# Rotated query tiles between the plain ones, the last attention-output tiles by token half, and the first gate and up products slice by slice

## The chip, the cores and the metric

The kernel runs on one core of a Trainium2 chip. The metric is the time of one execution on the device in microseconds (us). A core has five engines that run side by side, each through its own list of instructions in order: TensorE (PE, matmuls and the weight loads for them), VectorE (DVE), ScalarE (ACT), GpSimd (POOL) and SyncE (SP, which issues DMAs; ACT and POOL issue some too). They meet through semaphores. Matmuls write to PSUM, which has eight banks of 128x512 float32 here, and the other engines read them from there.

## The reference

One transformer block over 1024 tokens of width 1024, in float32: adaLN conditioning, one input projection, then two branches side by side (attention with a low-rank query and key/value, and a state-space scan), sigmoid gates, an output projection and a SwiGLU feed-forward network, each half closed by an RMS norm and a residual.

```python
q = (rms(q_lat) @ w_uq).reshape(s, 8, 64 + 32)
q_nope, q_rope = q[..., :64], rope(q[..., 64:])
kv = rms(kv_lat); k_nope = kv @ w_uk; v = kv @ w_uv
o = softmax(scale * (q_nope @ k_nope.T + q_rope @ k_rope.T)) @ v
branch_a = o @ w_attn_out
mixed = (gate_a * branch_a + gate_b * branch_b) @ w_mix_out
x = x + gt1 * rms(mixed)
h = rms(x) * (1 + sc2) + sh2
g, up = split(h @ w_ffn_in)
x = x + gt2 * rms((silu(g) * up) @ w_ffn_out)
```

## The kernel before

All activations lie transposed, features on the partitions and tokens along the row, and the 1024 tokens are worked on as two halves of 512. To keep float32 accuracy every operand is split in a high part (rounded to the matmul's float32 format) and a low part (the rest), and `mm3` (L197) issues three matmuls for one 128x128 weight block: high weight with high data, high weight with low data, low weight with high data. PE takes them in the order in which they are written.

Weights come through one stream, `WStream`. A list `wl` says in which order the matrices are used. SP loads them (`load`), ACT casts the high part and DVE subtracts for the low part (`split`, L183 and the next line), and `get(ahead=1, more=2)` hands out the next matrix, after it has put the split of the matrix behind it into ACT's and DVE's lists. So a matrix is split where the matrix before it is fetched, unless `get` is told to look further ahead. The order of all lists is written out by hand; nothing is reordered later.

**Query tiles.** The query projection has six 128-row tiles, in three pairs of one weight matrix each: four plain ones (`uq_nope(i, w)`) and two that hold the rotated part (`uq_rope`). A tile takes 18 matmuls (two halves of nine). Its halves stand in two PSUM banks, one of four named `mm` and one of four named `s`, taken in turn. A plain tile is evicted by `split_store`: ACT scales and rounds the high part (`sghi`), DVE makes the low part (`sglo`), and both go to DRAM; five pairs of these buffers are in turn. `uq_rope` evicts with twelve DVE products and sums against the tables `csb` and four `split_store`s. Around them stand three generators, moved on by `next`: `kv_norm` (applies the norm to the key/value rows, in two token halves), `krope` (the rotated key; its row `kr` comes by a DMA of POOL's) and `ych` (loads the state-space output in `ylo`, then takes gelu on ACT, a cast to `yhi` on ACT, and a subtraction on POOL, four times). Then key and value tiles alternate: `uk_half` in a bank `mm`, `uv_tiles` in a bank `s`, six matmuls each, sixteen of them. Before, the order is plain 0, 1, 2, 3, then rotated.

**Attention output.** For eight output tiles m and two token halves h, `ao_mm` accumulates twelve matmuls (for m < 4 nine of them ahead), and `ao_out` evicts: DVE multiplies with the gate `ga`, adds the other branch `mb`, ACT casts the high part into `mxt[h]`, POOL makes the low part. `ga` and `mb` of a tile (both halves) are loaded two tiles ahead by `gm_load` into two buffers. The mix projection follows: `mix_tile(0, 0)` reads all eight slices of `mxt[0]`.

**Feed-forward.** Hidden tiles come in pairs of matrices, gate `wg` and up `wu`. For a token half h, `ffn_in` runs `prod` over the eight slices k of `h2t[h]` for gate (24 matmuls), then for up (24), with `tick()` after every second slice (it moves on the work of a `chain` and issues waiting DMAs). The slices of `h2t[h]` are made one after another by `chain(h)`; `drain()` ends that chain just ahead of the first pair of each half, so its last slices are still being made on DVE and ACT while PE is at that pair:

```python
        drain()                     # the rest of chain(h): eight slices
...
        wg, wu = win.get(), win.get()
```

The first `get` here puts the split of `wu` behind the chain's last slice in ACT's and DVE's lists, the second that of the next pair's `wg`.

Of the kernel before, what the change touches and what calls it, by code (L numbers as in the profile page):

```python
# [17 lines left out]
P = 128  # L18
S = 1024
D = 1024  # L20
KD = D // P
HF = 512
# [35 lines left out]
class Ops:  # L58
# [6 lines left out]
    def tt(self, o, a, b, op):  # L65
        return self.eng.tensor_tensor(o, a, b, op=op)  # L66
# [24 lines left out]
def _body(tc, a, out):  # L91
# [53 lines left out]
    def flush(keep=0):  # L145
        while len(pending) > keep:
            A_.dma_start(*pending.pop(0))
# [49 lines left out]
    def mm3(ps, w, rhi, rlo, k, first, last):  # L197

        whi, wlo = w
        c = slice(k * P, (k + 1) * P)  # L200
        PE.matmul(ps, whi[:, c], rhi, start=first, stop=False)  # L201
        PE.matmul(ps, whi[:, c], rlo, start=False, stop=False)  # L202
        PE.matmul(ps, wlo[:, c], rhi, start=False, stop=last)  # L203
# [89 lines left out]
            units += [("in", p, hs) for p in range(starts[g], starts[g + 1])] + [("out", g, hs)]  # L293

    wl = [(a["win"][i], KD * P) for i in range(26)]
    wl += [(a["wuq"][i], 6 * P) for i in range(3)] + [(a["wuk"], 8 * P), (a["wuv"], 2 * HF)]
    wl += [(a["wglu"][m], 8 * P) for m in range(KD)]
    wl += [(a["wao"][m], KD * P) for m in range(4)]
    mix0 = len(wl)
# [7 lines left out]
    win = WStream(wp, wl, D, (2, 3))  # L307
# [558 lines left out]
    def lat_apply(raw, rc, gcol, hi, lo, al, mk_ps):  # L866

        dg = [al(h) for h in range(2)]
        for h in range(2):
            norm_diag(rc[:, 4 * h:4 * h + 4], dg[h])  # L870
        yield
        rs = [al(2), al(3)]
        for h in range(2):
            ps = mk_ps()
            PE.matmul(ps, ones, dg[h], start=True, stop=True)
            A_.copy(rs[h], ps)
        yield

        def low(h, k):
            tt(lo[k][:, halves[h]], raw[k][h], hi[k][:, halves[h]].bitcast(F32), ALU.subtract)  # L880

        prev = None
        for h, c in enumerate(halves):
            for k in range(len(raw)):
                r = raw[k][h]
                stt(r, r, gcol[:, k:k + 1], rs[h], ALU.mult, ALU.mult)
                A_.copy(hi[k][:, c], r)
                if prev:
                    low(*prev)
                prev = h, k  # L890
            if h == 0:
                yield
        low(*prev)

    def load_rows(i):
        t = nr_tile()
        SY.dma_start(t, pdram[i])
        return [t[:, c] for c in halves]
# [106 lines left out]
    def dense_tile(w, i, kk, hi_in, lo_in):  # L1005

        pss = []
        for h, c in enumerate(halves):
            ps = (ps_mm, ps_s5)[h]()
            for k in range(kk):  # L1010
                mm3(ps, w, hi_in[k][:, c], lo_in[k][:, c], i * kk + k, k == 0, k == kk - 1)
            pss.append(ps)
        return pss
# [13 lines left out]
    kv_norm = lat_apply([load_rows(3), load_rows(4)], kv_rc[0], g_kv, kvhi, kvlo, lambda i: kv_scr[i], ps_mm)  # L1027
# [38 lines left out]
    def uq_nope(i, w):  # L1066
        pss = dense_tile(w, i % 2, 3, qhi, qlo)
        for c, ps in zip(halves, pss):
            split_store(ps, SCALE, [qkd["qn"][e, i * P:(i + 1) * P, c] for e in range(2)])

    def uq_rope():

        w = win.get(2)
        pss = [dense_tile(w, i, 3, qhi, qlo) for i in range(2)]
        qr = [qkd["qr"][e].rearrange("(h a r) s -> a h r s", a=2, r=16) for e in range(2)]
        yield
        prev = []
        for h, c in enumerate(halves):
            for i, op in enumerate((ALU.subtract, ALU.add)):
                ti = rp.tile([P, HF], F32, name="qra", tag="qra", bufs=3)  # L1080
                u = rp.tile([P, HF], F32, name="qrb", tag="qrb")
                tt(ti, pss[i][h], csb[0][:, c], ALU.mult)
                tt(u, pss[1 - i][h], csb[1][:, c], ALU.mult)
                tt(ti, ti, u, op)
                prev.append((ti, SCALE, [qr[e][i][:, :, c] for e in range(2)]))
                if len(prev) > 1:
                    split_store(*prev.pop(0))
            yield
        for p in prev:
            split_store(*p)  # L1090
# [47 lines left out]

    ych, krope = y_chain(), k_rope()
    next(krope)  # L1140
    for i in range(4):
        if i % 2 == 0:
            w = win.get()
        uq_nope(i, w)
        next(kv_norm, None)
        if i == 2:
            next(krope)
        if i == 2:
            next(ych)
    uqr = uq_rope()  # L1150
    next(uqr)
    for _ in kv_norm:
        pass
    next(ych)
    for _ in uqr:
        next(ych)
    w = win.get()
    uv = uv_tiles(win.get())
    for m in range(4):
# [87 lines left out]
    def mx_ps():  # L1247
        return psat.tile([P, S], F32, name="mx", tag="mx")
# [74 lines left out]
    for i in range(len(steps) + LAG):  # L1323
        if 0 <= i < len(steps):
            h, kt = steps[i]
# [4 lines left out]
        if NJ <= j < len(steps):  # L1330
            mh_, mt = steps[j]
            ps = mx_ps()
# [39 lines left out]
    def ps_b():  # L1372
        return psb.tile([P, HF], F32, name="mm", tag="mm")
# [5 lines left out]
    with ExitStack() as m_es:  # L1379
        mp = pool("mp", bufs=2, stack=m_es)  # L1380
        gm = {}

        def gm_load(m):
            if m < KD:
                gm[m] = [mp.tile([P, S], F32, name=n, tag=n) for n in ("ga", "mb")]
                later(gm[m][0], gdram[KD + m])
                later(gm[m][1], mbd[m])

        def ao_mm(ps, w, m, h, ks):
            o = m % 2 * 4  # L1390
            for k in ks:
                c = slice((o + k) * P, (o + k + 1) * P)
                for wi, x in ((0, ohi), (0, olo), (1, ohi)):
                    PE.matmul(ps, w[wi][:, c], x[k][:, halves[h]], start=(k == 0 and x is ohi and wi == 0),
                              stop=(k == 3 and wi == 1))

        def ao_out(ps, m, h):
            c = halves[h]
            ga, mb = gm[m]
            t = mp.tile([P, HF], F32, name="t", tag="t", bufs=4)  # L1400
            tt(t, ps, ga[:, c], ALU.mult)
            ao_low()
            tt(t, t, mb[:, c], ALU.add)
            A_.copy(mxt[h][0][:, m, :], t)  # L1404
            mlast.append((t, m, h))

        def ao_low():

            if mlast:
                t, m, h = mlast.pop()  # L1410
                hi, lo = mxt[h]
                G.tensor_tensor(lo[:, m, :], t, hi[:, m, :].bitcast(F32), op=ALU.subtract)

        mlast = []

        gm_load(0)
        gm_load(1)
        flush()
        w = [win.get(), win.get()]
        pss = {}  # L1420
        for m in range(4):
            for h in range(2):
                pss[m, h] = ps_b()
                ao_mm(pss[m, h], w[m // 2], m, h, range(3))
        for m in range(KD):
            if m >= 4 and m % 2 == 0:
                w = [win.get()]
            if m in (2, 4):
                win.split()
            for h in range(2):  # L1430
                if m < 4:
                    ps = pss[m, h]
                    ao_mm(ps, w[m // 2], m, h, (3,))
                else:
                    ps = ps_b()
                    ao_mm(ps, w[0], m, h, range(4))
                ao_out(ps, m, h)
            gm_load(m + 2)
            flush()
        ao_low()  # L1440
    o_es.close()
    v_es.close()
# [20 lines left out]
    def tick():  # L1463
        flush(FK)
        while backlog:
            try:
                next(backlog[0])
                return
            except StopIteration:
                backlog.pop(0)  # L1470
# [6 lines left out]
    def prod(ps, w, hi, lo, n, off=0):  # L1477
        for k in range(n):
            mm3(ps, w, hi(k), lo(k), off + k, k == 0, k == n - 1)
            if k % 2:  # L1480
                tick()

    def half_tile(pl, nm, bufs=None, n=HF):
        return pl.tile([P, n], F32, name=nm, tag=nm, bufs=bufs or 2)
# [114 lines left out]
    def ffn_in(p, hs):  # L1599
        wg, wu = win.get(), win.get()  # L1600
        if p not in ft:
            ft[p] = tuple(fp.tile([P, S], F32R, name=n, tag=n, bufs=5) for n in ("fhi", "flo"))
        for h in hs:
            c = halves[h]
            pg, pu = ps_b(), ps_b()
            hi, lo = h2t[h]
            for w, ps in ((wg, pg), (wu, pu)):
                prod(ps, w, lambda k: hi[:, k, :], lambda k: lo[:, k, :], KD)
            t = fp.tile([P, HF], F32, name="silu", tag="silu", bufs=2)
            A_.activation(t, pg, AF.Silu)  # L1610
            tt(t, pu, t, ALU.mult)
            fh, fl = ft[p]
            A_.copy(fh[:, c], t)  # L1613
            tt(fl[:, c], t, fh[:, c].bitcast(F32), ALU.subtract)
# [51 lines left out]
    for u, (kind, i, hs) in enumerate(units):  # L1666
# [14 lines left out]
        if i < last:  # L1681
            for m in range(KD):
                if m % 2 == 0:
                    w = win.get()
# [15 lines left out]
        for c0, n in ((0, HF),) if hs == (0,) else ((0, QF), (QF, QF)):  # L1700
            h = hs[0]
# [115 lines left out]
```

## Time and profile before

| | us |
|---|---|
| median of 3 runs | 1683.53 (1682.95 to 1684.88) |
| the profiled execution | 1684.47 |
| its span in the trace | 1682.7 |
| PE busy in it | 1618.4 (96%) |
| DVE busy | 977.7 (58%) |
| ACT busy | 552.5 (33%) |
| POOL busy | 164.0 (10%) |

The span runs from the first to the last instruction of the profiled execution; 1.8 us of its time lie around it. "Idle before" in a row is time in which an engine stood still ahead of an instruction, and what it waited for. The granted clock is the share of 2.4 GHz that TensorE was given: 1.00, or 0.50 for 1.2 GHz. The stretches that the change touches are the query tiles (408 to 465 us of the span), the attention output and the start of the mix (776 to 837), and the first pair of the feed-forward network for each half (922 to 941 and 998 to 1011).

### The profile page before, as it was taken

The page shows a single profiled execution, that of the slowest core. Times are in us where ns is not written, and L with a number is a line of the kernel's source. Part 1 is how long each engine was busy: PE and PEld are TensorE (multiplying, and loading weights), DVE is VectorE, ACT ScalarE, POOL GpSimd, SP SyncE. Part 2 cuts the span into 40 slices and gives each one's busy share as a digit, 9 for nine tenths or more (in the row PEclk, how much of TensorE's full clock was granted, in tenths as well). Part 3 has the DMA queues.
Part 4 walks back from the last instruction along what each step waited for, and adds up shares of the span by engine and source line. Part 5 has one row for each costly group of instructions (what it writes and reads, how often), then busy time and mean ns, then how long its engine had stood idle before and what let it go on. Part 6 is the DMA issues. An engine that isn't in the chain of part 4 may idle for free.

```text
span 1682.7 us, 19415 instructions
## 1 busy us (share of the span) xinstructions
PE 1618.4 (96%) x7454; PEld 1309.0 (78%) x7454; DVE 977.7 (58%) x1615; ACT 552.5 (33%) x743; POOL 164.0 (10%) x221
## 2 busy tenths in 40 slices
PE   6989999999899999999999999999999999999995
PEld 6878888888688677767777778888888888888874
DVE  6978898977857778854636763223223222323366
ACT  4142322223531467763334443211111121121233
POOL 0430000012220000000524200000000000000002
PEclk9899999999999999999999999999999999999998
DMA  8143333567987424202523442212111111111243
GB/s 330 63 124 100 108 103 94 157 218 221 310 244 223 104 63 101 45 14 67 196 94 107 162 135 91 73 66 79 59 63 51 50 51 50 51 41 48 80 142 129
DMA packets 90748, 189.66 MB, mean 113 GB/s; under 512 B 19992, under 2 KB 36504, under 8 KB 90656
## 3 DMA queue, kind: packets, MB, share of 16 engines
q1 hardware_dynamic: 57920, 120.62, 23.7%
q10 hardware_dynamic: 27104, 49.95, 8.6%
q0 software_dynamic: 5632, 17.86, 3.5%
q8 instruction: 58, 0.95, 0.2%
q14 instruction: 34, 0.28, 0.1%
HBM read 148.61 MB, written 39.78 MB: 112 GB/s over the span
## 4 chain that ended last, share of the span: by engine, by line
PE 65%; DVE 20%; ACT 5%; DMA 4%; issue 4%; ACTq 1%; SPq 0%; DVEq 0%; POOLq 0%
PE mm L203 17%; PE mm L202 17%; PE mm L201 17%; DVE t L66 5%; DVE wlo L66 2%; PE sc L1255 1%; PE sc L1256 1%; PE sc L1257 1%; PE pv L1281 1%; PE pv L1280 1%; PE pv L1282 1%; ACT whi L183 1%; DMA mxd<-mneg 1%; PE mx L1203 1%; DVE s L695 1%
## 5 line engine op out<-in xcount | busy, mean ns | idle before, releaser
L202 PE MATMUL mm<-mh,whi 128*128 128x512 f32 x736 | 289.3, 393 | 4.8 <-DVE mh L74 3.1
L201 PE MATMUL mm<-mh,whi 128*128 128x512 f32 x736 | 289.8, 394 | 0.8 <-ACT mh L1404 0.5
L203 PE MATMUL mm<-mh,wlo 128*128 128x512 f32 x736 | 288.7, 392 | 1.7 <-DVE wlo L66 1.6
L66 DVE TENSOR_TENSOR wlo<-wraw,whi 128x1024 fp32r<-128x1024 f32 (+1 forms) x128 | 155.8, 1235 | 80.2 <-ACT whi L183 80.1
L66 DVE TENSOR_TENSOR silu<-mm,silu 128x512 f32<-128x512 f32 x44 | 30.4, 692 | 277.4 <-PE mm L203 271.2
L183 ACT CAST whi<-wraw 128x1024 fp32r<-128x1024 f32 (+1 forms) x128 | 129.9, 1036 | 149.0 <-PE mm L202 137.0
L202 PEld LDWEIGHTS mm<-mh,whi 128*128 128x128 f32 x736 | 139.2, 189 | 38.2 <-DVE mh L74 6.6
L203 PEld LDWEIGHTS mm<-mh,wlo 128*128 128x128 f32 x736 | 139.2, 189 | 32.9 <-DVE wlo L66 4.3
L201 PEld LDWEIGHTS mm<-mh,whi 128*128 128x128 f32 x736 | 139.2, 189 | 31.1 <-ACT whi L183 0.9
L201 PE MATMUL mm<-hhi,whi 128*128 128x512 f32 x384 | 156.7, 408 | 1.5 <-ACT ev L604 1.5
L202 PE MATMUL mm<-hlo,whi 128*128 128x512 f32 x384 | 152.8, 398 | 1.4 <-DVE hlo L74 1.4
L203 PE MATMUL mm<-hhi,wlo 128*128 128x512 f32 x384 | 153.5, 400 | 0.0
L201 PE MATMUL mm<-fhi,whi 128*128 128x512 f32 x304 | 118.8, 391 | 0.0
L202 PE MATMUL mm<-flo,whi 128*128 128x512 f32 x304 | 118.5, 390 | 0.0
L203 PE MATMUL mm<-fhi,wlo 128*128 128x512 f32 x304 | 118.3, 389 | 0.0
L66 DVE TENSOR_TENSOR mr<-mm,mr 128x512 f32<-128x512 f32 (+1 forms) x88 | 56.3, 641 | 97.1 <-PE mm L203 97.0
L66 DVE TENSOR_TENSOR plo<-p,phi 128x1024 fp32r<-128x1024 f32 x64 | 78.3, 1224 | 40.0 <-ACT phi L1261 39.6
L1613 ACT CAST fhi<-silu 128x512 fp32r<-128x512 f32 x44 | 27.3, 621 | 222.2 <-DVE silu L66 222.2
L201 PEld LDWEIGHTS mm<-hhi,whi 128*128 128x128 f32 x384 | 73.3, 191 | 19.6 <-ACT ev L604 1.9
L202 PEld LDWEIGHTS mm<-hlo,whi 128*128 128x128 f32 x384 | 73.1, 190 | 18.5 <-DVE hlo L74 1.8
L1260 ACT ACTIVATE p<-sc 128x1024 f32<-128x1024 f32 x64 | 65.7, 1026 | 64.5 <-PE sc L1257 64.5
L203 PEld LDWEIGHTS mm<-hhi,wlo 128*128 128x128 f32 x384 | 73.0, 190 | 17.9 <-DVE wlo L66 0.2
(524 smaller groups left out, 2938.7 us busy)
## 6 DMA issues: line engine op xcount, KB each, us to landing
wraw<-in_wfi SPq DMA_DIRECT2D x58, 512.0 KB
wraw<-in_win SPq DMA_DIRECT2D x26, 512.0 KB
wraw<-in_wfo SPq DMA_DIRECT2D x20, 512.0 KB
gdram<-ev ACTq DMA_DIRECT2D x32, 256.0 KB
wada<-in_wada POOLq DMA_DIRECT2D x15, 512.0 KB, 4.3
wraw<-in_wmix SPq DMA_DIRECT2D x10, 512.0 KB
xT<-in_xT SPq DMA_DIRECT2D x8, 512.0 KB
pw<-in_wadk SPq DMA_DIRECT2D x8, 512.0 KB
```

Source lines behind the costliest of these rows:

```text
L66: return self.eng.tensor_tensor(o, a, b, op=op)
L183: A_.copy(hi, t)
L201: PE.matmul(ps, whi[:, c], rhi, start=first, stop=False)
L202: PE.matmul(ps, whi[:, c], rlo, start=False, stop=False)
L203: PE.matmul(ps, wlo[:, c], rhi, start=False, stop=last)
L695: V.tensor_tensor_scan(t[64:P, 511::-1], r[64:P, ::-1], z[i][64:P, ::-1], 0.0, op0=ALU.mult, op1=ALU.add)
L1203: PE.matmul(pieces[j], qt["qhi"][b][0:96, t * P:(t + 1) * P], qt["khi"][b][0:96, halves[j]], start=True, stop=True)
L1255: PE.matmul(ps[:, c], kh[0:97, kc], qh[0:97, c], start=True, stop=False)
L1256: PE.matmul(ps[:, c], kh[0:96, kc], ql[0:96, c], start=False, stop=False)
L1257: PE.matmul(ps[:, c], kl[0:96, kc], qh[0:96, c], start=False, stop=True)
L1260: A_.activation(p, ps, AF.Exp)
L1613: A_.copy(fh[:, c], t)
```

## The change

1. The rotated query tiles are computed after the plain tiles 0 and 1; their eviction, and all of `kv_norm`, are written ahead of the plain tiles 2 and 3. The two later weight matrices change places in `wl`. The look-ahead of two (`get(2)`) stays with the third matrix fetched: there the splits of the key and value matrices are written, now behind the rotated eviction and ahead of the plain tiles 2 and 3. The first steps of `krope` and `ych` stand right behind the rotated matmuls, the later steps of `ych` behind the plain tiles.
2. The last two attention-output tiles are done as (6,0), (7,0), (6,1), (7,1) in place of (6,0), (6,1), (7,0), (7,1).
3. For the first pair (p == 0), `prod2` goes through the slices once and issues three gate and three up matmuls for each, with a `tick()` after each slice.

```diff
-    wl += [(a["wuq"][i], 6 * P) for i in range(3)] + [(a["wuk"], 8 * P), (a["wuv"], 2 * HF)]
+    wl += [(a["wuq"][i], 6 * P) for i in (0, 2, 1)] + [(a["wuk"], 8 * P), (a["wuv"], 2 * HF)]
...
     def uq_rope():
-        w = win.get(2)
+        w = win.get()
...
-    for i in range(4):
-        if i % 2 == 0:
-            w = win.get()
+    w = win.get()
+    for i in range(2):
         uq_nope(i, w)
-        next(kv_norm, None)
-        if i == 2:
-            next(krope)
-        if i == 2:
-            next(ych)
+        next(kv_norm)
     uqr = uq_rope()
     next(uqr)
+    next(kv_norm)
+    next(krope)
+    next(ych)
     for _ in kv_norm:
         pass
+    for _ in uqr:
+        pass
+    w = win.get(2)
+    for i in range(2, 4):
+        uq_nope(i, w)
+        next(ych)
     next(ych)
-    for _ in uqr:
-        next(ych)
...
-        for m in range(KD):
-            if m >= 4 and m % 2 == 0:
+        order = [(m, h) for m in range(KD - 2) for h in range(2)]
+        order += [(m, h) for h in range(2) for m in range(KD - 2, KD)]
+        for m, h in order:
+            if h == 0 and m in (4, 6):
                 w = [win.get()]
...
-            gm_load(m + 2)
-            flush()
+            if h and m < KD - 2:
+                gm_load(m + 2)
+                flush()
...
+    def prod2(pss, ws, hi, lo):
+        for k in range(KD):
+            for ps, w in zip(pss, ws):
+                mm3(ps, w, hi[:, k, :], lo[:, k, :], k, k == 0, k == KD - 1)
+            tick()
...
-            for w, ps in ((wg, pg), (wu, pu)):
+            if p == 0:
+                prod2((pg, pu), (wg, wu), hi, lo)
+            for w, ps in ((wg, pg), (wu, pu)) if p else ():
                 prod(ps, w, lambda k: hi[:, k, :], lambda k: lo[:, k, :], KD)
```

## Rows read from the trace of the kernel before

**Rows 1.** The page, busy time, share of the span and instructions by engine.
```profile
PE 1618.4 (96%) x7454; PEld 1309.0 (78%) x7454; DVE 977.7 (58%) x1615; ACT 552.5 (33%) x743; POOL 164.0 (10%) x221
```

**Rows 2.** Waits of PE over the span: us in total, times, longest.
```profile
PE s L1105 <- DVE qra L66: 5.2, 1, 5.2
PE mm L202 <- DVE mh L74: 3.1, 5, 1.4
PE mm L202 <- POOL mh L1412: 1.7, 1, 1.7
```

**Rows 3.** Stretches: length, busy by engine (instructions), PEclk the granted clock.
```profile
446.75:451.17 4.42, 4.42 (x11) 3.48 (x11) 4.26 (x4) 3.62 (x6) 2.62 (x1) 0.50 0.52 196
...
829.60:837.00 7.40, 6.78 (x16) 4.83 (x17) 3.08 (x3) 2.42 (x4) 1.18 (x1) 0.54 0.43 142
```

**Rows 4.** Timeline: ACT, then PE (matmuls 1, 27, 48), first pair, half 1.
```profile
1003.23 1.99 ACT L183 CAST whi<-wraw 128x1024 fp32r<-128x1024 f32 x2
...
997.81 0.39 PE L201 MATMUL mm<-mh,whi 128*128 128x512 f32 x1
...
1005.58 0.50 PE L203 MATMUL mm<-mh,wlo 128*128 128x512 f32 x1 [0.22 <-DVE wlo L66]
...
1010.48 0.39 PE L203 MATMUL mm<-mh,wlo 128*128 128x512 f32 x1
```

**Rows 5.** Timeline of PE, the first pair, half 0: matmuls 1, 25, 48 of 48.
```profile
922.04 0.39 PE L201 MATMUL mm<-mh,whi 128*128 128x512 f32 x1
...
932.65 0.40 PE L201 MATMUL mm<-mh,whi 128*128 128x512 f32 x1
...
938.85 0.39 PE L203 MATMUL mm<-mh,wlo 128*128 128x512 f32 x1
```

**Rows 6.** Timeline of ACT, the first pair, half 0.
```profile
929.84 0.72 ACT L1570 ACTIVATE mh<-ht,ada 128x512 fp32r<-128x512 f32 x1 [0.73 <-DVE ht L74]
...
930.47 1.03 ACT L183 CAST whi<-wraw 128x1024 fp32r<-128x1024 f32 x1
```

**Rows 7.** Timeline of DVE, the same stretch.
```profile
923.02 0.75 DVE L74 SCALAR_TENSOR_TENSOR mh<-ht,ada,mh 128x512 fp32r<-128x512 f32 x1
...
928.27 0.75 DVE L74 SCALAR_TENSOR_TENSOR mh<-ht,ada,mh 128x512 fp32r<-128x512 f32 x1
...
931.53 2.36 DVE L66 TENSOR_TENSOR wlo<-wraw,whi 128x1024 fp32r<-128x1024 f32 x2 [0.18 <-ACT whi L183]
```

**Rows 8.** Timeline of PE, query, key and value tiles.
```profile
434.62 0.39 PE L201 MATMUL mm<-kvhi,whi 128*128 128x512 f32 x1
...
446.75 0.80 PE L1105 MATMUL s<-whi,kvhi 128*128 128x512 f32 x1 [5.17 <-DVE qra L66]
```

**Rows 9.** Timeline of DVE, query tiles.
```profile
419.81 0.96 DVE L66 TENSOR_TENSOR wlo<-wraw,whi 128x768 fp32r<-128x768 f32 x1 [1.75 <-ACT whi L183]
...
434.92 0.68 DVE L66 TENSOR_TENSOR qra<-mm,cs 128x512 f32<-128x512 f32 x1
...
438.16 2.64 DVE L66 TENSOR_TENSOR qra<-qra,qrb 128x512 f32<-128x512 f32 x1
```

**Rows 10.** Instructions on the rotated key's row `kr`: its DMA.
```profile
L1051 POOL DMA_DIRECT2D kr<-pdram x1: 597/597/597, 412.4 to 412.4; - x1
...
DMA to landing us min/median/max: 11.6/11.6/11.6
```

**Rows 11.** Timeline of POOL, DVE and PE, start of the mix.
```profile
826.12 4.66 POOL L1412 TENSOR_TENSOR mh<-t,mh 128x512 fp32r<-128x512 f32 x3
826.63 0.68 DVE L66 TENSOR_TENSOR t<-mm,ga 128x512 f32<-128x512 f32 x1
...
827.35 1.05 DVE L66 TENSOR_TENSOR t<-t,mb 128x512 f32<-128x512 f32 x1
...
830.03 1.83 DVE L66 TENSOR_TENSOR wlo<-wraw,whi 128x1024 fp32r<-128x1024 f32 x1 [0.40 <-ACT whi L183]
...
831.92 0.80 PE L203 MATMUL mm<-mh,wlo 128*128 128x512 f32 x1 [0.62 <-DVE wlo L66]
```

More of the change, by code (lines that the diff above doesn't have):

```diff
@@ L1424, in _body @@
                 ao_mm(pss[m, h], w[m // 2], m, h, range(3))
-        for m in range(KD):
-            if m >= 4 and m % 2 == 0:
+        order = [(m, h) for m in range(KD - 2) for h in range(2)]
+        order += [(m, h) for h in range(2) for m in range(KD - 2, KD)]
+        for m, h in order:
+            if h == 0 and m in (4, 6):
                 w = [win.get()]
-            if m in (2, 4):
+            if h == 0 and m in (2, 4):
                 win.split()
[L1430 to L1437, printed above, removed]
-            gm_load(m + 2)
-            flush()
+            if m < 4:
+                ps = pss[m, h]
+                ao_mm(ps, w[m // 2], m, h, (3,))
+            else:
+                ps = ps_b()
+                ao_mm(ps, w[0], m, h, range(4))
+            ao_out(ps, m, h)
+            if h and m < KD - 2:
+                gm_load(m + 2)
+                flush()
         ao_low()
```

## The prediction, as it was made before the change was run

> **What bounds the kernel now.** I read the page first: TensorE is busy in 96% of the span and no other engine in more than 58% [rows 1]. So the time is the number of matmuls times their spacing, plus the holes in TensorE's list. The change adds and removes no matmul; it can only open, close or move holes. I then read TensorE's waits: three of them belong to the places that the diff touches, 5.2 us for the eviction of the rotated query tiles, 3.1 us in five pieces for slices of `h2t`, 1.7 us for the last low part of `mxt` [rows 2]. Third, the stretches with the granted clock, because a hole is dearer than it looks: after the 5.2 us hole, eleven matmuls took 4.42 us at a granted clock of 0.50 (1.2 GHz); after the broken stretch at 826 us sixteen took 7.40 at 0.54 [rows 3]. At full clock 21 matmuls start in 4.90 us [rows 4], so one costs 0.23. The first stretch thus lost 4.42 - 11 x 0.23 = 1.9 us, the second 7.4 - 16 x 0.23 = 3.7, of which some 0.5 was waiting; I take 3.2. Last I read timelines of the three places engine by engine, for what each list does in the order of the code.
>
> **Gate and up slice by slice, first half.** This is where the time will change most. Before, PE does 24 gate matmuls, held up by the slices (they start at 922.04, the 25th matmul, the first with `wu`, at 932.65), then 24 of up [rows 5]. That `wu` is late too, only nobody notices: its cast stands in ACT's list behind the cast of the chain's last slice (929.84) and runs 930.47 to 931.50 [rows 6], its low part is the first half of two subtractions that start at 931.53, so it ends near 932.7 [rows 7]. The gate product has covered this. After the change the fourth matmul already needs `wu`. The order on ACT and DVE is not changed (both `get`s still stand behind `drain()`), and neither waits for PE there. So PE does three gate matmuls to 922.7 and stands until 931.5, 8.8 us. Behind the waiting matmul are queued the other 21 gate matmuls, whose data arrive meanwhile, and everything after; the silu and the norm sums of the next chain wait for those.
>
> The sum: the sixth matmul needs the low part and runs at 932.8; before, the 27th ran at 932.65 + 2 x 0.23 = 933.1. That is 21 matmuls fewer, 21 x 0.23 = 4.8, less 0.3: 4.5 us. The clock will have fallen; of a slow stretch of 4.42 us, 1.2 are spent waiting for the low part anyway, and 3.2 us hold seven matmuls that lose 0.2 each: 1.5. Together **+6.0**. Bounds: no fall of the clock, 4.5; the long slow stretch, 4.5 + 3.2 = 7.7.
>
> The ticks keep their number (eight per half) and their places after matmuls 36 and 48, so the next chain moves on as before, and the silu stands behind its work in ACT's list as before: nothing.
>
> **The same, second half.** Gate starts at 997.81. The cast of `wu` is the first of two from 1003.23, so it is ready at 1004.25; its low part let matmul 27 go at 1005.58, after a wait of 0.22 [rows 4]. After the change the sixth matmul goes at that time: 21 x 0.23 = 4.8. The hole from 998.5 to 1004.25 is longer than the 5.2 us one that cost the clock, so again 3.1 us at half speed, 1.5. **+6.3**; bounds 4.8 and 8.0.
>
> The Trainium skill (TensorE: Matmul & The Clock Gate, the table at its head) gives PE a queue of 64 with a "partial reorder window". Read as one in which matmuls may pass a waiting one, it would let the remaining gate matmuls fill the hole, and these two terms would be near 0 instead of +12.3. The trace speaks against that reading: in the 5.2 us hole [rows 2] no later matmul was run ahead. I keep it as a rival.
>
> **Rotated tiles between the plain ones.** PE's order of query tiles keeps 36 + 36 matmuls, so it reaches the key tiles at 434.62 as before [rows 8]. Before, it then does five key and value tiles and stands until 446.75, because the third value tile needs the bank of a rotated half. Afterwards that bank is free in time; what is late next is the key weights, whose split now stands behind the rotated eviction.
>
> DVE's list: the split of the third query matrix ends at 420.8 [rows 9]; half 0 of `kv_norm`, five operations of 0.68, to about 423; then the rotated key's row, whose DMA, issued at 412.4, lands 11.6 later at 424.0 [rows 10], so DVE waits, and goes on to 424.8; half 1 of the norm to 428.2; then twelve products and sums and four splits, 16 x 0.65 = 10.4, to 438.6. Before, two of these were stretched to over 2.6 by POOL's subtractions (2.64 at 438.16, against 0.68) [rows 9]; POOL's subtractions now come later, so I count none. ACT's last rotated cast ends near 437.9, its cast of the key weights (1.03) near 438.9, DVE's low part 1.2 later at 440.1. PE stands from 434.6 to 438.9 and again to 440.1: as long as before, only earlier. With 28 matmuls left to the point where it was at 446.75, it comes there at 440.1 + 28 x 0.23 = 446.5, or 448.4 with a slow stretch of 1.9; before, that point was at 446.75 with its slow stretch still ahead, 448.65. A gain of 0.2 to 2.1 at that point. But ahead of the first key tile's eviction ACT still has two weight casts, three gelus with their casts, eight operations at 1.03 [rows 6], four plain halves of half that width and a table load: 8.2 + 2.1 and the load, so past 450. With the subtraction that follows on DVE the bank comes free near 452.5 to 453.9, and PE needs it at about 452. I take **0**: from -3 (the key's row lands early enough not to hold DVE) to +1.5 (the four loads of `ylo`, now issued a tile earlier, delay it, and POOL's subtractions fall on the plain splits).
>
> On that last point the trace and the skill can be set against row 438.16. The DVE product that reads PSUM took 0.68 while POOL was at work, the sum beside it that reads only SBUF took 1.05 [rows 11]. The Trainium skill (SBUF — State Buffer, "Who interferes with whom") says the same as a rule: DVE collides with GpSimd's reads when both its inputs are in SBUF. The plain splits read PSUM. By the rule they would cost nothing more; priced like 438.16, four times 2.0 on DVE. I go by the row that reads PSUM, so by neither does the term move beyond its upper bound.
>
> The two query matrices that change places are of one size and are split at the same places: nothing, covered by the 8 us of matmuls of the tiles before.
>
> **Attention output by token half.** The low part of slice 7 comes a tile earlier, by some 1.5 us, so the 1.7 us wait mostly goes. But PE's next wait is the low weights of mix tile 1, ready only when the DVE operation 830.03 + 1.83 ends; PE goes on at 831.92 [rows 11]. That operation stands behind the same 16 evictions in DVE's list, so the gain is given back 2 us later. It can be worse: tile (7,0) is evicted one place earlier and needs its `ga` and `mb`, loaded just ahead. **+0.4**, from -0.5 to +1.2. The loads and their flush stay at the same places (none is left after tile 5): nothing.
>
> **Sum.** 6.0 + 6.3 + 0 + 0.4 = +12.7. The profiled execution took 1684.47 (a span of 1682.7 and 1.8 around it); with 12.7 it is 1697.2. The median of the runs is 1683.53, 0.9 less, so I expect a median of **1696**. The bounds added up: -3 - 0.5 + 4.5 + 4.8 = +5.8, so 1689; and +1.5 + 1.2 + 7.7 + 8.0 = +18.4, so 1702.
>
> **Rivals.**
>
> A, faster: `wu` is ready at the pair's start, because some earlier `get` or `split` has run ahead. Then slice by slice does what it looks like: a slice gives PE 1.4 us of work where slices come in (928.27 - 923.02)/3 = 1.75 us [rows 7], and the loss of the gate product, 932.65 - 922.04 - 24 x 0.23 = 5.1, goes, and in the second half 1005.58 - 997.81 - 26 x 0.23 = 1.8 [rows 4]. 1683.5 - 6.9 + 0.4 = 1677. It decides from the point where the cast of `wu` ends ahead of the gate's fourth matmul, 922.7; the break-even lies about halfway, near 927. Against it stands the cast at 930.47 right behind the last slice [rows 6], in a list whose order is written out. Chance 0.08.
>
> B, slower by less: the query stage closes its hole wholly (5.2 and the slow stretch, 1.9), if DVE is some 5 us ahead of my list. For it: DVE no longer waits for store buffers. Against it: the key weights behind the rotated eviction. 1696 - 7.1 = 1689. Chance 0.12.
>
> C, no change: PE lets ready matmuls pass the waiting one, and the wait for `wu` costs nothing: 1684. Against it the 5.2 us hole. Chance 0.03.
>
> My forecast has the remaining 0.77.
>
> **How the numbers follow.** About 0.2% (3.4 us) is what a measurement of this kernel can tell from no change. Slower by more: the forecast and most of B (1689 is +5), 0.87. Faster: A, 0.08. Same: C and the low end of B, 0.05. The range goes from 1687.5 (B) to 1700.5 and leaves out A, C and the far ends of the bounds.
>
> **What would show it.** In the changed trace: a wait of PE for the cast of a feed-forward weight, some 8.8 us, a few matmuls into the first pair of half 0, and one of 5 to 6 us in half 1, each followed by a granted clock near 0.5; the wait for slices of `h2t` nearly gone; in the query stage a wait for the key weights near 435 us in place of the one for `qra` at 441; at the mix, mix tile 1 waiting for its low weights near 832 as before. The prediction is wrong if PE runs through the first pair without a wait of several us, or if the query stage ends more than 3 us earlier.

## The result and the profile after

The changed kernel takes **1698.17 us** (median of 4 runs, 1694.93 to 1698.37), the one before 1684.2 us beside it (4 runs, 1682.95 to 1688.41): a ratio of **1.0074**, 95% interval 1.0052 to 1.0096. It is slower by 14.0 us by the medians and by 12.5 by the means, on which the ratio rests; the forecast was 1696 with a range of 1687.5 to 1700.5. The profiled execution took 1698.37 us with a span of 1696.2, 13.5 longer than that of before.

Where it went can be read without guessing, since the same matmuls run in both kernels. I took the start of the matmul at which each stage begins and compared the lengths of the stages, one profiled execution of each kernel. "Spread pair" stands for the two matmuls that spread a norm's row `rs` (L266), the last step of a norm ahead of its use:

| Stage, from and to (starts on PE) | before | after | difference | forecast |
|---|---|---|---|---|
| first query matmul to first matmul of the gated unit | 56.41 | 57.39 | +0.98 | 0 |
| from there through attention and attention output to the first mix matmul | 356.90 | 357.18 | +0.28 | - |
| first mix matmul to the second spread pair behind it | 88.53 | 88.88 | +0.35 | +0.4 |
| from there to the third spread pair (holds the first gate and up pair of half 0) | 29.21 | 35.19 | **+5.98** | +6.0 |
| third spread pair to the first gate matmul of half 1 | 58.42 | 58.42 | 0 | 0 |
| first gate matmul of half 1 to the next output projection | 45.54 | 51.63 | **+6.09** | +6.3 |
| the rest, to the last spread pair | 627.01 | 626.90 | -0.11 | - |

The differences add up to 13.6 us, the spans differ by 13.5: nothing is missing. That the stages with unchanged code came out this close in these two executions is luck; in others the attention alone differs by up to 7 us (last section).

The page of the changed kernel, busy time by engine. PE does the same 7454 matmuls and is busy for only 0.4 us longer than in [rows 1]; the other 13.1 us of the longer span are time in which it stands. (A slow stretch counts as busy; the kernel before had its own, at other places.)

```profile
PE 1618.8 (95%) x7454; PEld 1311.2 (77%) x7454; DVE 971.9 (57%) x1615; ACT 552.4 (33%) x743; POOL 164.8 (10%) x221
```

PE's waits in the changed kernel, over the whole span (total, times, longest):

```profile
PE mm L201 <- ACT whi L183: 16.0, 4, 8.6
...
PE mm L201 <- issue: 4.5, 1, 4.5
...
PE mm L201 <- DVE sglo L74: 2.2, 2, 2.0
```

Set beside [rows 2], the row for `qra` (5.2) and that for slices of `h2t` (3.1 in five pieces) are gone. In their place stand waits for the cast of a weight, line 183, with a longest of 8.6 us, a wait of 4.5 in the query stage, for which the view names no releaser ("issue"), and one of 2.0 for the low half of a key tile. Here is the large one, in the timeline of PE, ACT and DVE, the first pair of half 0 (start, length; in brackets the idle time before and its releaser):

```profile
923.65 0.39 PE L201 MATMUL mm<-mh,whi 128*128 128x512 f32 x1
...
932.05 1.03 ACT L183 CAST whi<-wraw 128x1024 fp32r<-128x1024 f32 x1
...
933.11 2.36 DVE L66 TENSOR_TENSOR wlo<-wraw,whi 128x1024 fp32r<-128x1024 f32 x2 [0.18 <-ACT whi L183]
...
933.13 0.79 PE L201 MATMUL mm<-mh,whi 128*128 128x512 f32 x1 [8.63 <-ACT whi L183]
...
934.39 0.80 PE L203 MATMUL mm<-mh,wlo 128*128 128x512 f32 x1
...
946.43 0.39 PE L203 MATMUL mm<-mh,wlo 128*128 128x512 f32 x1
```

PE does three gate matmuls, then stands 8.63 us until the cast of the up weights ends. The 4th starts at 933.13, the 6th at 934.39, as soon as the low part is there, the 48th at 946.43. Only three of the 24 gate matmuls stand ahead of the first up matmul; the other 21 stand behind it. In half 1 the same picture, PE alone:

```profile
1005.40 0.39 PE L201 MATMUL mm<-mh,whi 128*128 128x512 f32 x1
...
1011.90 0.80 PE L201 MATMUL mm<-mh,whi 128*128 128x512 f32 x1 [5.66 <-ACT whi L183]
...
1013.16 0.80 PE L203 MATMUL mm<-mh,wlo 128*128 128x512 f32 x1
```

And the stretches of the changed kernel, each hole with what follows it (columns as in [rows 3]: length, busy time of PE, PEld, DVE, ACT and POOL, then the granted clock; the DMA share and GB/s are last):

```profile
434.50:439.32 4.82, 0.27 (x2) 0.03 (x1) 4.40 (x8) 2.29 (x4) 0.00 (x0) 0.98 0.85 252
439.32:442.70 3.38, 3.35 (x7) 2.23 (x8) 3.38 (x4) 3.35 (x5) 0.00 (x0) 0.52 0.53 204
...
924.40:933.10 8.70, 0.09 (x1) 0.00 (x0) 8.26 (x11) 5.42 (x9) 1.36 (x1) 0.66 0.13 47
933.13:937.50 4.37, 4.33 (x9) 3.00 (x10) 2.34 (x2) 0.89 (x1) 0.00 (x0) 0.50 0.87 275
1006.10:1011.90 5.80, 0.14 (x1) 0.00 (x0) 5.39 (x9) 4.09 (x7) 0.00 (x0) 0.77 0.04 16
1011.90:1016.20 4.30, 4.26 (x10) 2.92 (x11) 2.34 (x2) 0.90 (x1) 0.00 (x0) 0.52 0.37 125
```

Each hole is paid twice: after the two of the feed-forward nine and ten matmuls take 4.4 and 4.3 us, after that of the query stage seven take 3.4, at a granted clock of 0.50 to 0.52 (1.2 GHz). It is the stretch of [rows 3] again, at a new place. And during the 8.7 us hole DVE is busy for 8.26: PE waits for the list that makes the slices, and the weights stand at its end.

### The profile page after: what moved, and what is told of

Its sections match the earlier page's. It is cut to its first block, busy times and chain, and to the rows that moved or that the text cites. A ratio compares the mean times of both kernels' runs of the same rounds, so it can differ in the third digit from the quotient of the medians.

```text
span 1696.2 us, 19414 instructions
## 1 busy us (share of the span) xinstructions
PE 1618.8 (95%) x7454; PEld 1311.2 (77%) x7454; DVE 971.9 (57%) x1615; ACT 552.4 (33%) x743; POOL 164.8 (10%) x221
## 4 chain that ended last, share of the span: by engine, by line
PE 65%; DVE 19%; DMA 6%; ACT 5%; issue 3%; SPq 1%; ACTq 0%; DVEq 0%; POOL 0%; POOLq 0%
PE mm L203 17%; PE mm L201 17%; PE mm L202 16%; DVE t L66 5%; DVE wlo L66 2%; PE sc L1257 2%; PE sc L1258 1%; PE sc L1259 1%; PE pv L1283 1%; PE pv L1282 1%; PE pv L1284 1%; ACT whi L183 1%; DMA mxd<-mneg 1%; PE mx L1205 1%; DVE mr L66 1%
## 5 line engine op out<-in xcount | busy, mean ns | idle before, releaser
L202 PEld LDWEIGHTS mm<-hlo,whi 128*128 128x128 f32 x384 | 73.2, 191 | 16.7 <-issue 0.2
```

## The experiments

**The slices out, the slices alone.** My theory: the loss is the slice order's alone. The first kernel takes it out of the changed one, the second puts it alone into the kernel before.

```diff
-            if p == 0:
-                prod2((pg, pu), (wg, wu), hi, lo)
-            for w, ps in ((wg, pg), (wu, pu)) if p else ():
+            for w, ps in ((wg, pg), (wu, pu)):
```

> The changed kernel with gate and up product one after the other again (the other two parts stay). Theory (the loss comes from the up weights that are split too late for the slice order): the two waits of 8.6 and 5.7 us for the high part of the up weights and the slow clock behind them go, about 12 us less than the changed kernel: 1686, 1 to 2 above the kernel before, what the other two parts cost. Rival (the query stage or the attention output owns the loss): it stays above 1692.

Measured: 1689.18 (10 runs, 1682.98 to 1699.01) against 1687.11 of the kernel before on that chip, ratio 1.0013 (0.9995 to 1.0032). The first pair's stages are back at 29.05 and 45.53 us.

```diff
+    def prod2(pss, ws, hi, lo):
...
-            for w, ps in ((wg, pg), (wu, pu)):
+            if p == 0:
+                prod2((pg, pu), (wg, wu), hi, lo)
+            for w, ps in ((wg, pg), (wu, pu)) if p else ():
```

> The kernel before with the slice order of the first pair alone. Theory: 6.0 and about 6 us of new loss in the two halves, 1696, with PE waiting 8.6 and 5.7 us for the high part of the up weights. Rival (the parts only cost together): under 1690.

Measured: 1697.92 (4 runs), ratio 1.007 (1.0044 to 1.0097), the two stages 34.72 and 51.35. So this one part, alone, costs what the whole change costs, and without it the change can't be told from no change. PE's wait in its first pair of half 0 is the same 8.63 us, with its own timeline row:

```profile
932.69 0.79 PE L201 MATMUL mm<-mh,whi 128*128 128x512 f32 x1 [8.63 <-ACT whi L183]
```

**The up weights split early.** If the hole is the late split and not the order of the products, then a split of the up weights ahead of the last slices should turn the loss into the gain of my rival A. `get(2)` puts two matrices' splits into the lists instead of one, so the up weights' split comes with the gate weights':

```diff
-        w = kept.pop(m) if h and m in kept else win.get()
+        w = kept.pop(m) if h and m in kept else win.get(2 if h and m == KEEP0 - 1 else 1)
...
-                    w = win.get()
+                    w = win.get(2 if i == 0 and hs == (0,) and m == KD - 2 else 1)
```

> The changed kernel, but the up weights of the first pair are split where the gate weights are, ahead of the chain's last slices, by a look-ahead of two at the matrix fetched just before; the arithmetic is the same. Theory: the two waits go, and slice by slice now does what it looks like: a slice gives PE 1.4 us of work and comes every 1.5 us or so, so nearly all of the 12 us comes back and the 7 us that the kernel before lost in its gate product shrink by 4 to 6: 1680 to 1682. Rival (the slice order itself costs, by its change of weights and of PSUM bank after every three matmuls): the two waits go but the spacing of the matmuls is over 0.24 us, and the time is at 1686 or above.

Measured: 1685.88 (12 runs), ratio 0.9995 (0.9982 to 1.0009). The two stages: 26.62 and 43.52 us, together 16.7 less than in the changed kernel and 4.6 less than before. Its rows, ACT and then the stretch of the first pair (columns as above), then all of PE's waits from 915 to 1050 us:

```profile
923.79 1.99 ACT L183 CAST whi<-wraw 128x1024 fp32r<-128x1024 f32 x2
```

```profile
916.00:942.00 26.00, 24.04 (x106) 18.52 (x104) 19.89 (x32) 12.89 (x19) 3.98 (x3) 1.00 0.33 104
```

```profile
PE mm L266 <- DVE rs L66: 1.5, 1, 1.5
PE mm L202 <- DVE mh L74: 0.7, 1, 0.7
PE mm L203 <- DVE wlo L66: 0.4, 2, 0.2
```

Both casts now stand together, ahead of the last slices, and the granted clock stays at 1.00. The hole is gone with the split's place alone, and the order slice by slice, with its weights on hand, is a gain. It is smaller than rival A's 6.9, and the waits that are left come to 2.6 us: above all, PE reaches the third spread pair early and waits 1.5 us for the row `rs`, which DVE makes behind the slices and a weight's low part. The whole time missed my expectation: of the gain against before, 4.6 us in these two stages, less 0.5 and 0.8 that its query stage (56.95) and the start of its mix (89.29) show above before's, the interval allows at most 3.0. Its attention stage, unchanged code, ran 217.77 us against 213.17; more on that below.

**The early split alone**, in the kernel before, with the products one after the other:

> Control to the one with the early split: the kernel before with that early split alone, gate and up one after the other. Theory: the gate product still waits for the slices, which the split pushes back by 1.2 us, and the up weights were not missed before: no change to 1.5 us slower, 1684 to 1686. Rival (the early split alone is worth something, whatever the order of the products): 3 us or more faster.

Measured: 1688.38 (12 runs), ratio 1.0013 (0.9995 to 1.0031); the two stages 29.93 and 46.18, that is +0.7 and +0.6. So neither the early split nor the slices gain by themselves: the split early costs 1.3 us, the slices alone cost 11.3 (5.5 + 5.8), together they save 4.6.

**The query stage, three tries.** It came out at +1, not at 0. The kernels with one run, here and at the mix, are read by their stages alone: they took 1707.71, 1702.55 and 1704.15 us here, 1702.85 and 1686.61 at the mix, but in code that none of them changes the first query matmul came between 405.2 and 413.5 us and the attention took 214.2 to 219.1. The first kernel takes the wait for the key weights away by splitting them a matrix earlier, in `uq_rope`:

```diff
-        w = win.get()
+        w = win.get(2)
```

> The changed kernel, but the key weights are split ahead of the rotated eviction, not behind it (a look-ahead of two one fetch earlier); the value weights stay behind it. Read from the stretch between the first query matmul and the first matmul of the gated unit, 57.4 us in the changed kernel and 56.4 before. Theory (behind the late weights, the list of ACT is the next limit: three gelus stand ahead of the first key tile's eviction): the first key tile runs at once near 434.5, PE then waits for the value weights, the wait for a bank near 452 grows by what was saved, and the stretch stays within 0.5 us of 57.4. Rival (the late key weights are the whole cost): the stretch falls by 1.4 us or more.

One run: the query stage took 58.13, against 57.39 of the changed kernel, outside the half microsecond that I had allowed. The key tiles no longer wait, but PE waits for the value weights instead:

```profile
444.36 0.79 PE L1105 MATMUL s<-whi,kvhi 128*128 128x512 f32 x1 [4.80 <-ACT whi L183]
```

That nothing is gained was expected, and the wait for the value weights too; but the wait of the fifth key tile for a PSUM bank (2.01 us in the changed kernel), which should have grown by what was saved, fell to 1.63.

The second kernel drops the `next(ych)` behind each of the plain tiles 2 and 3, so that two gelus with their casts leave ACT's list ahead of the key tiles' evictions:

```diff
     for i in range(2, 4):
         uq_nope(i, w)
-        next(ych)
     next(ych)
```

> The changed kernel with one gelu, not three, ahead of the key and value tiles; the other three stand behind the first three key tiles, one each. The same stretch. Theory (ACT's list holds back the first evictions, and the bank they free): the first key tile is evicted 4 us earlier, near 446 in place of 450.5, the 2.0 us wait of PE for that bank goes, and the stretch falls by 1.5 to 2.5 us, to about 55.4. Rival (POOL's subtractions and DVE set the pace, so the order on ACT doesn't matter): it stays within 0.5 us of 57.4; or the last gelu now comes too late for the gated unit and PE waits there for its last slice by as much.

One run: the query stage fell to 56.44, by 1.0 and not by the 1.5 to 2.5 of my theory, and the bank's wait fell to 0.22, so the gelus with what follows them are what delays that eviction. But, as the second half of the rival had it, the stage behind it, gated unit to scores, grew from 98.81 to 106.39, since the gated unit now waits for its own input, with these two rows of PE at its start and a dozen matmuls at half pace behind them:

```profile
466.38 0.50 PE L201 MATMUL mm<-yhi,whi 128*128 128x512 f32 x1 [2.36 <-ACT yhi L1040]
...
468.81 0.79 PE L202 MATMUL mm<-ylo,whi 128*128 128x512 f32 x1 [1.93 <-POOL ylo L1045]
```

One microsecond won, 7.6 lost: a net loss of 6.6.

The third moves `next(krope)` behind the plain tiles 2 and 3, so that DVE doesn't wait for the row `kr` ahead of the rotated eviction:

```diff
-    next(krope)
...
+    next(krope)
```

> The changed kernel, but the sign step of the rotated key on DVE, which waits 1.7 us for its row's DMA, stands behind the query tiles and no longer ahead of the second half of the norm. Read from the first query matmul to the first of the gated unit (57.4 us in the changed kernel, 56.4 before). Theory (the chain is this DMA, DVE's norm and rotated eviction, then ACT's list): everything behind moves 1.7 to 2.4 us earlier, PE's wait for the key weights and the bank wait shrink, the stretch is 55 to 56. Rival (another queue takes over at once): over 57.

One run: 56.85, half of a microsecond less, where my theory wanted 1.4 to 2.4; kernels whose query stage is that of the changed one gave 56.95 to 57.39, so this is hardly a gain. The key tiles do start earlier, 28.4 us after the first query matmul in place of 31.0. But ACT then waits 1.31 us for the DMA of the gated unit's weights, and the bank's wait grows from 2.01 to 3.84:

```profile
451.51 1.04 ACT L183 CAST whi<-wraw 128x1024 fp32r<-128x1024 f32 x1 [1.31 <-DMA wraw<-in_wglu]
```

```profile
454.68 0.50 PE L201 MATMUL mm<-kvhi,whi 128*128 128x512 f32 x1 [3.84 <-DVE sglo L74]
```

Neither my theory nor its rival came out so. In all three kernels most or all of what one wait gives up, or more, comes back at the next, within 20 us.

**The start of the mix.** The change takes little there because PE's next wait is mix tile 1's weights. This kernel puts their split ahead of the last four evictions:

```diff
-            if h == 0 and m in (2, 4):
+            if h == 0 and m in (2, 4, 6):
                 win.split()
```

> The changed kernel, but the weights of mix tile 1 are split ahead of the last four evictions of the attention output, not behind them. Read from the stretch from the first mix matmul to the second spread matmul pair of the norms (88.9 us in the changed kernel, 88.5 before). Theory (the earlier low part gains nothing because the next wait, for these weights, ends at the same time): the waits of 1.4 and 0.7 us for them go, the wait for slice 7 grows by 1 to 1.5 us since the evictions come later, and the clock hardly falls: the stretch shortens by 2 to 4 us. Rival (the evictions set the end and the weights only fill their shadow): it stays within 0.7 us.

One run: the mix stage took 84.22 us, 4.7 less than in the changed kernel (I had expected 2 to 4) and 4.3 less than before. The two waits left, and the stretch around them:

```profile
837.08 0.50 PE L202 MATMUL mm<-mh,whi 128*128 128x512 f32 x1 [1.14 <-POOL mh L1414]
838.77 0.50 PE L202 MATMUL mm<-mh,whi 128*128 128x512 f32 x1 [0.71 <-POOL mh L1414]
```

```profile
834.00:846.00 12.00, 10.14 (x44) 7.72 (x43) 7.64 (x10) 5.50 (x10) 6.36 (x4) 1.00 0.17 50
```

The same split, with the old order of the tiles (in the kernel before, `if m in (2, 4, 6): win.split()`):

> The kernel before with the early split of the weights of mix tile 1 alone, the output tiles in their old order. Read from the first mix matmul to the second spread pair (88.5 us before, 84.2 with new order and early weights). Theory (the order by token half is worth what it brings forward slice 7's low part once the weights no longer wait behind it): the wait for slice 7 is 1 to 2 us longer than in the new order and may cost the clock, the stretch is 86 to 87. Rival (the order is worth nothing even then, the early weights are all): 84.2 as well.

One run: 88.67, no gain over 88.53, where I had expected 86 to 87. The weights are no longer late, but with the old order the slices of `mxt[0]` are, in three pieces, and the clock falls:

```profile
829.35 0.50 PE L202 MATMUL mm<-mh,whi 128*128 128x512 f32 x1 [1.09 <-POOL mh L1412]
830.55 0.50 PE L201 MATMUL mm<-mh,whi 128*128 128x512 f32 x1 [0.47 <-ACT mh L1404]
...
832.71 0.79 PE L202 MATMUL mm<-mh,whi 128*128 128x512 f32 x1 [1.65 <-POOL mh L1412]
```

```profile
833.30:839.00 5.70, 5.70 (x15) 4.44 (x14) 1.22 (x1) 2.02 (x3) 0.60 (x1) 0.51 0.12 29
```

So the attention output by token half is worth some 4.5 us once the weights are there (88.67 here, 84.22 above), and nothing before; the early weights are worth nothing without it. This pair behaves as the slices and the early split do.

**Put together.** First all of it on the changed kernel, early up weights, early mix weights and the dropped gelus:

> The early split of the up weights, one gelu ahead, and the early mix weights together, with all three parts of the change. Theory: against the kernel before, the feed-forward pairs gain 4.6 (as measured with the early split), the query stage loses 1 and gains 2, the mix start gains 2: some 6 to 8 us faster than before, 1676 to 1678 where before is at 1684, a ratio near 0.996. Rival (what is saved in the early stages is lost at the start of the attention or in the mix, which wait for other things): the ratio stays between 0.998 and 1.001.

Measured: 1687.55 (12 runs) against 1690.3, ratio 0.9986 (0.9969 to 1.0004). The stages: mix 84.48, the first pairs 26.65 and 43.52, as in the single kernels; but the gated unit's 105.55, 6.7 more than before, eats most of it, and the expected 6 to 8 us did not come: the rival held. So the last kernel keeps the query stage of before, and takes from the change only the two parts that gain once their weights are there:

> A version meant to beat both: the query stage of the kernel before, the attention output by token half with the weights of mix tile 1 split ahead of the last evictions, and the slice order with the up weights split early. Theory: the stretch from the first mix matmul to the second spread pair at 84.3 us (88.5 before) and the two feed-forward pairs at 26.7 and 43.5 (29.2 and 45.5): 8.7 us faster than before, a ratio near 0.995. Rival (the saved time is lost again in later waits): within 0.2% of before.

Measured: **1681.8** (12 runs, 1678.1 to 1685.97) against 1688.03 on the same chip, ratio **0.9968** (0.9952 to 0.9983). It beats the kernel before by 0.3%, and with that the changed one, which is 0.7% above it. Its stages: query 56.34, mix 84.08, the first pairs 26.64 and 43.52, by which it should gain 9.1 us; the interval is 2.9 to 8.1, so some of that did not arrive (last section). PE's waits from 820 to 1060 us, all that are left:

```profile
PE mm L202 <- POOL mh L1412: 1.7, 2, 1.0
PE mm L266 <- DVE rs L66: 1.5, 1, 1.5
PE mm L202 <- DVE mh L74: 0.7, 1, 0.7
PE mm L203 <- DVE wlo L66: 0.3, 1, 0.3
```

## Why the prediction held, step by step

**Half 0, +6.0.** Measured 5.98, and the mechanism as forecast: a hole of 8.63 us (forecast 8.8), the sixth matmul waiting on the low part, the granted clock at 0.50 after it. The terms hold too. From the sixth matmul to the last it is 946.43 - 934.39 = 12.0 us for 42 matmuls, which at 0.23 are 9.7. Of the 2.4 us over, 0.9 belongs to eight small matmuls that stand inside the product in both kernels, the norm sums of the next chain (one row of before, one of the changed kernel):

```profile
935.40 0.95 PE L245 MATMUL mm<-ones,acc 128*128 128x1 f32 x8
```

```profile
942.99 0.95 PE L245 MATMUL mm<-ones,acc 128*128 128x1 f32 x8
```

They are why the up product of before, 932.65 to 938.85, is 0.9 longer than 23 x 0.23 [rows 5], though it ran at a granted clock of 1.00. The first stretch here is of before, the second of the changed kernel, from its sixth matmul on:

```profile
932.65:939.24 6.59, 6.58 (x33) 5.21 (x31) 3.72 (x14) 0.00 (x0) 0.00 (x0) 1.00 0.64 207
```

```profile
934.39:937.53 3.14, 3.14 (x8) 2.51 (x9) 1.08 (x1) 0.00 (x0) 0.00 (x0) 0.50 0.86 277
```

In that slow stretch seven matmuls start in 3.1 us and lose 1.5, as forecast. So 4.8 - 0.3 + 1.5 = 6.0. The first and second runs put the whole loss on this part; the third shows that it is the split's place.

**Half 1, +6.3.** Measured 6.09; the hole was 5.66 us (forecast 5.75), the clock 0.52 behind it, and the slow stretch cost 1.4 of the 1.5 that were forecast.

**Attention output, +0.4.** Measured 0.35 for the stage, but the three profiled kernels with the code of before in it gave 87.0 to 88.5 and the six with that of the change 88.5 to 89.3, so its size is known only to about a microsecond. The wait for the last low part went only from 1.7 to 1.3, and as forecast the gain was given back at mix tile 1's weights, whose low part PE could use 10.5 us after the first mix matmul, 10.3 before:

```profile
831.59 0.73 PE L201 MATMUL mm<-mh,whi 128*128 128x512 f32 x1 [1.42 <-ACT whi L183]
...
833.45 0.79 PE L203 MATMUL mm<-mh,wlo 128*128 128x512 f32 x1 [0.71 <-DVE wlo L66]
```

That this is what stands in the way, the run with the early mix weights shows: 4.7 us.

**Query stage, 0 (-3 to +1.5).** Measured +0.98, and kernels with the old order spread from 56.1 to 57.2 in this stage, those with the new one from 56.95 to 57.4; call it half to one microsecond; the ranges overlap. The order of events is the forecast's: the wait for `qra` is replaced by one for the key weights, to 439.32 (forecast 438.9), and for their low part to 440.54 (440.1), then a slow stretch. PE's row names no releaser, but the first of two casts on ACT ends there, and the kernel that splits the key weights earlier has no such wait:

```profile
438.19 1.98 ACT L183 CAST whi<-wraw 128x1024 fp32r<-128x1024 f32 x2
...
439.32 0.76 PE L201 MATMUL mm<-kvhi,whi 128*128 128x512 f32 x1 [4.55 <-issue]
```

What was mis-sized is the end of it, the bank. DVE's list there, and PE's wait for the last of its rows:

```profile
445.13 0.69 DVE L74 SCALAR_TENSOR_TENSOR sglo<-mm,sghi 128x512 fp32r<-128x512 f32 x1 [2.31 <-ACT sghi L1020]
...
450.64 2.90 DVE L66 TENSOR_TENSOR wlo<-wraw,whi 128x1024 fp32r<-128x1024 f32 x1 [4.22 <-ACT whi L183]
453.46 0.68 DVE L74 SCALAR_TENSOR_TENSOR sglo<-mm,sghi 128x512 fp32r<-128x512 f32 x1
...
454.20 0.50 PE L201 MATMUL mm<-kvhi,whi 128*128 128x512 f32 x1 [2.01 <-DVE sglo L74]
```

POOL subtracts from 444.69 to 447.09 and from 447.69 to 452.46. The plain splits cost nothing more by that: the one at 445.13, which reads PSUM, took 0.69 inside POOL's first subtraction. There the trace agrees with the Trainium skill's rule (SBUF — State Buffer, "Who interferes with whom") that a DVE instruction with at most one SBUF input, outside the two-port modes, does not contend with GpSimd. But I asked this only of the plain splits. The subtraction for the low part of the gated unit's weights reads SBUF alone, stands just ahead of the eviction, and took 2.90 us. The same operation of the kernel before, where POOL was idle from 450.88 to 457.98:

```profile
451.35 1.21 DVE L66 TENSOR_TENSOR wlo<-wraw,whi 128x1024 fp32r<-128x1024 f32 x1
```

Those 1.7 us are the difference between a bank that comes free at 452.5 and one that comes free at 454.2, and PE waited 2.01 for it. That is worked out from the rows; the run with two gelus fewer shows that with their work, and POOL's that follows it, out of the way, the wait is down to 0.22.

**The rivals.** A (weights ready early) did not occur in the changed kernel and does in the one with the early split; it is worth 4.6, not 6.9, since the row `rs` is late next. B (the query stage closes its hole) fell: the bank took back what the key weights' earlier wait gave. C (ready matmuls pass a waiting one) fell: 21 gate matmuls with their weights on hand stood behind one for 8.63 us, with slices arriving all the while. So the reading of the table in the Trainium skill (TensorE: Matmul & The Clock Gate, at its head) that I had weighed is not borne out here. It is not the page's own either: the same row of the table names weight loads as what is pulled ahead of matmuls in flight.

## What to carry to other kernels

An order that uses a second operand earlier asks for more than the data it was made for: look up in the lists of the engines that prepare that operand where it becomes ready, and move that too. Here three matmuls of cover took the place of 24, which cost 12 us, and a split moved along with it made 4.6 us of gain out of the same edit. And where two inputs are late by about the same, removing either shows nothing: name the next wait and remove both in one run before calling an edit worthless.

## What was not expected of the hardware

DVE's subtraction of 128x1024, both inputs in SBUF, took 2.90 us beside POOL's subtractions and 1.21 without them. In the whole trace of the changed kernel the 112 such subtractions away from POOL's took 1.22 to 1.23 us, the nine that overlap one 1.34 to 2.90, while operations of DVE that read PSUM kept their 0.68 to 0.69 beside POOL.

Waits of 1.09, 0.47 and 1.65 us within five microseconds were followed by a granted clock of 0.51 for fifteen matmuls, with no single hole over 1.7 us; after two of 1.14 and 0.71 it stayed at 1.00.

The attention stage (first score matmul to the first of the attention output), the same code in all kernels, took 212.0 to 219.1 us in thirteen profiled executions. Most of that is the granted clock. The shortest, of the kernel without the slice order, then the longest, of the one with the early key weights:

```profile
563.37:775.34 211.97, 205.26 (x871) 154.66 (x871) 154.26 (x139) 145.26 (x149) 3.41 (x7) 0.99 0.22 49
```

```profile
568.81:787.93 219.12, 210.91 (x871) 158.21 (x871) 154.23 (x139) 145.19 (x149) 3.43 (x7) 0.96 0.22 48
```

Of the 7.15 us between them 5.65 are PE's busy time for the same matmuls, at a granted clock of 0.99 and 0.96. The rest is mostly PE's wait for the small transfers through `mxd`, which goes from 3.8 us (the changed kernel, 213.47) to 6.0 (the kernel with early mix weights, 217.19). Why the clock falls in one execution and not in another was not followed.

This bears on the last kernel's 9.1 us. In its profiled execution the attention took 217.97 us against 213.17 of the profile of before, 3.9 of the 4.8 in PE's busy time, and the first query matmul came 2.2 us later, so the spans differ by 2.3 only (1680.4 and 1682.7). The kernel before was profiled on the first chip alone. Its median there is 1684.2 us from four runs, and 1687 to 1690 from 17 to 29 runs on each of three others, where it went from 1680 to 1696; whether the chips differ is not shown. How much of the gap between the 9.1 us by the stages and the 2.9 to 8.1 by the interval is the clock stays open.
